# One plain pair fewer in front of the seven-product feed-forward, a new opening order, and an embedding unit moved behind it

## The chip, the cores and the metric

The kernel runs on one core of a Trainium2 chip. The metric is device time in microseconds (us): 2044.14 us, the median of 3 runs (2043.42 to 2046.07). TensorE multiplies (PE in the profile; its weight loads are PEld), VectorE (DVE), ScalarE (ACT) and GpSimd (POOL) do the element-wise work, SyncE (SP) issues most transfers.

## The reference, cut to what matters

One layer of a decoder trunk on 1024 prompt tokens and 64 sample tokens, model width 1024. After two mixing branches and an output projection come the feed-forward and an embedding term:

```
x = x + merged @ w_o
up = rmsnorm(x, g_ffn) @ w_up              # 1024 -> 2*3072
gate, val = split(causal_dwconv3(up))
x = x + (gelu(gate) * val) @ w_down        # 3072 -> 1024
e = rmsnorm(p @ w_ple, g_ple)              # p: 256 wide, known from the start
x = x + sigmoid(x @ w_ple_gate) * e
```

## The kernel before, in words

Channels lie on the partitions, tokens along the rows. The tokens are done in two halves, one whole layer after the other: the first has 512 prompt tokens, the second 512 prompt and 64 sample tokens (576, in two groups of 288). Each fp32 product is made of three fp32r products, high by high, high by low and low by high; so every weight block (128x128) gives three matmuls per group of tokens.

Weights come in units of 1024 columns (eight blocks), in an order fixed in the list `ORDER`. Each unit is loaded five units ahead by SP (`load`), and two units ahead ACT makes its high part (`split_hi`, tile whi, L324) and DVE its low part (`split_lo`, tile wlo, L329); `hook` issues these three from inside the unit that is being multiplied.

The feed-forward has 24 pairs f of a gate block and a value block. `PLAN` gives the order of its work, as a list that `ffn_plan` writes out:

- ("ple", j): half of the embedding product p @ w_ple, one unit. Each of its four results is copied out by ACT, stored to DRAM by a DMA that ACT issues, squared by ACT, and the square is added to a running sum by POOL (`j_ple`, `square`, L442). After unit 1 a job starts (`stat_later`) that turns the sum into a row of reciprocal roots with two small groups of matmuls (L453, L487) and DVE work between them (L468, L478).
- ("up", u): one up-projection block done plainly, one unit of 8 x 3 matmuls per group. A plain pair is two such units.
- ("step", f, p): product p of 7 of pair f. The pairs after the first PLAIN are done by a scheme for 2x2 block matrices with seven products instead of eight: the two blocks of weights (gate, value) by two halves of the input channels on one side, two halves of the channels by two halves of the tokens on the other. A step is half a unit (4 blocks, 12 matmuls over half of the tokens); two steps share a unit. Products 1 and 2 take the weights as they are, and rows of the normalised input as they are (b11, b21). The products 3, 5, 6 and 7 need sums of weights (made early in DRAM by `make_sums`), and 4 to 7 need sums of the input (t1 to t4, made by the job `operands`).
- ("down", d): one unit of the down-projection, 19 of them among the steps, the last five behind them.

Jobs (`Job`) are Python generators that are advanced by one `tick` after each block of a whole unit and after each second block of a step; what a job issues is put into the queues of the engines in this order, and each engine works its queue in order. At the start of the feed-forward three of them run beside the matmuls: `stat2` (waits 8 ticks, then L453, 6 ticks, L468 and L478, 7 ticks, L487), `operands` (starts at tick 10, four rounds of 11 ticks, DVE L1121 to L1125 and L1107, ACT L1115, L1119 and L1105), and for each finished up-block `j_up`: the evacuation on DVE (L503, or L505 to L507 in the second half), one tick later a first tap of the convolution on ACT (L529), two ticks later two more on DVE (L533).

In `step`, product 1 starts a PSUM bank, and when its four blocks are issued ACT copies the bank to a row (L1181); product 2 is then added into the same bank by the matmuls, so it has to follow that copy. In the order before, product 2 is the last of its pair.

Of the kernel before, what the change touches and what calls it, by code (L numbers as in the profile page):

```python
# [48 lines left out]
def paired(a, b, lead):  # L49
    o = [(a, m) for m in range(lead)]  # L50
    for m in range(8):
        o.append((b, m))
        if m + lead < 8:
            o.append((a, m + lead))
    return o
# [9 lines left out]
SUMS = ("s1", "s2", "s3", "s4")  # L65
CHUNK = 4

PLAIN = 4


def ffn_plan():

    plan, steps, down = [("ple", 0), ("ple", 1)], 0, 0
    plan += [("up", s * FF + f) for f in range(PLAIN) for s in range(2)]
    for f in range(PLAIN, FF):
        todo = [(f, 1), (f, 6)] + [(f - 1, 3)] * (f > PLAIN) + [(f, p) for p in (7, 5, 4, 2)]
        ready = min(f - 4, down + 2)
        for i, x in enumerate(todo):
            plan.append(("step", *x))
            steps += 1  # L80
            while i >= len(todo) - 2 and steps % 2 == 0 and down < ready:
                plan.append(("down", down))
                down += 1
    plan.append(("step", FF - 1, 3))
    assert steps % 2
    return plan, down


PLAN, DOWNS = ffn_plan()


def slot_order(hf):

    o = [("lx", m) for m in range(8)]
    o += [("q", i) for i in range(4)] + [("k", i) for i in range(4)]
    o += [("v", i) for i in range(8)]
    o += [("lg", m) for m in range(8)]
    o += paired("ga", "ya", LEAD_A)
    o += [("rg", m) for m in range(8)]
    o += paired("gb", "yb", LEAD_B)  # L100
    o += [("wo", m) for m in range(8)]
    first = None
    for what, *x in PLAN:
        if what != "step":
            o.append((what, *x))
        elif first is None:
            first = tuple(x)
        else:
            o.append(("halves", first, tuple(x)))
            first = None  # L110
    assert first is None
    o += [("down", f) for f in range(DOWNS, FF)]
    o += [("gate", m) for m in range(8)] * (1 + hf)
    return o


ORDER = slot_order(0) + slot_order(1)
NU = len(ORDER)
PACKED = [(n, i) for n, c in (("lx", 8), ("q", 4), ("k", 4), ("v", 8), ("lg", 8), ("ga", 8), ("ya", 8), ("rg", 8), ("gb", 8), ("yb", 8), ("wo", 8)) for i in range(c)]
# [19 lines left out]
class Job:  # L139
# [7 lines left out]
    def step(self):  # L147
        try:
            self.wait += next(self.gen) or 1
        except StopIteration as e:  # L150
            self.done, self.val = True, e.value
# [16 lines left out]
class Trunk:  # L168
# [974 lines left out]
    def step(self, H, X, prep, rb, P, f, p):  # L1143

        nc = self.nc
        n = H.T // 2
        if self.half is None:
            i, h = self.cur, 0
            self.cur += 1
            self.half = i  # L1150
        else:
            i, h = self.half, 1
            self.half = None
        assert ORDER[i][0] == "halves" and ORDER[i][1 + h] == (f, p)
        s = P.setdefault(f, {})
        chain = {1: "a", 2: "a", 3: "c", 5: "c"}.get(p, p)
        if chain not in s:
            s[chain] = self.ps_new(1)[0]
            first = True
        else:  # L1160
            first = False
        bank = s[chain]
        out = bank[:, 0:n]
        xs = X[PRODUCTS[p][1]]
        for kk in range(4):
            b = 4 * h + kk
            while len(xs) <= kk:
                prep.step()
            xh, xl = xs[kk]
            wh, wl = self.whi[i % RING][:, b], self.wlo[i % RING][:, b]  # L1170
            mm = nc.tensor.matmul
            mm(out, lhsT=wh, rhs=xh, start=first and kk == 0, stop=False, skip_group_check=True)  # L1172
            mm(out, lhsT=wh, rhs=xl, start=False, stop=False, skip_group_check=True)  # L1173
            mm(out, lhsT=wl, rhs=xh, start=False, stop=kk == 3, skip_group_check=True)  # L1174
            if kk % 2:
                self.tick()
            self.hook(i, b)
        V = nc.vector
        if p == 1:
            s["row"] = self.new()  # L1180
            nc.scalar.copy(s["row"][:, 0:n], out)  # L1181
            return
        row = s["row"]
        r1, r2 = row[:, 0:n], row[:, n:2 * n]
        if p == 2:
            s["xg"] = self.new(wide=True)
            self.prefix(H, s["xg"], self.stf[:, f], 2)
            s["c11"] = self.start(self.j_first(H, rb, s["xg"], s.pop("a")))
        elif p == 6:
            V.tensor_add(r2, out, r1)  # L1190
            self.ps_rel([s.pop(6)])
        elif p == 7:
            V.tensor_add(r1, out, r2)
            self.ps_rel([s.pop(7)])
        elif p == 5:
            s["v"] = self.new()
            V.scalar_tensor_tensor(s["v"][:, n:2 * n], out, -1.0, r1, op0=ALU.mult, op1=ALU.subtract)
        elif p == 4:
            V.tensor_sub(s["v"][:, 0:n], out, r1)  # L1199
            self.ps_rel([s.pop(4)])  # L1200
            xv = self.new(wide=True)
            self.prefix(H, xv, self.stf[:, FF + f], 2)
            s["val"] = self.start(self.j_value(H, rb, s["v"], xv, FF + f))
        else:
            V.tensor_add(r2, out, r2)  # L1205
            self.ps_rel([s.pop("c")])
            gate = self.start(self.j_gelu(H, rb, row, s["c11"], s["xg"], f))
            s["hp"] = self.start(self.j_val(H, s["val"], gate), delay=6 if f == FF - 1 else 9)
# [181 lines left out]
    def run(self, H, res, nxt):  # L1390
# [10 lines left out]
        first = None if H.hf else self.first_units(H, xn, res["w"])  # L1401
# [27 lines left out]
        for g in range(4):  # L1429
            banks = self.ps_new(len(H.chunks))  # L1430
            for j in range(2):
                i = self.begin(("v", 2 * g + j))
# [97 lines left out]
        emb = None  # L1530
        for what, *x in PLAN:
            if what == "step":
                if x == [PLAIN, 1]:
                    prep.get()
                    self.rel(x1p[:4])
                    for r in x1p[4:]:
                        for name, h in (("b21", slice(0, n)), ("b22", slice(n, T))):
                            X[name].append(tuple(y[:, h] for y in r.get()))
                self.step(H, X, prep, rb, P, *x)
            elif what == "up":  # L1540
                self.up(H, *x, x1p, rb, P)
            elif what == "ple":
                self.ple(H, *x, pp, esum)
                if x == [1]:
                    emb = self.start(self.stat_later(H, esum), delay=10)
            else:
                self.down(H, *x, P, x1)
# [23 lines left out]
        for i, g in enumerate(parts):  # L1571
# [4 lines left out]
            first = self.gates_abreast(x2p, groups) if i == 0 else []  # L1576
# [307 lines left out]
```

## Time and profile before

| what | value |
|---|---|
| median of 3 runs | 2044.14 us |
| the profiled execution's own time | 2044.08 us |
| its span, first to last instruction | 2042.3 us |
| PE busy | 2022.4 us, 99% |
| DVE, ACT, POOL busy | 1444.7, 908.7, 580.8 us |
| chain that ended last: PE, DVE, ACT, POOL | 88%, 6%, 2%, 0% |
| TensorE clock granted, mean | 0.996 of full |

The profile is one execution. Busy matmuls overlap, so the time that a matmul takes from PE is read from the distance between starts. The first half's feed-forward begins about 498 us into the span, the second's about 1530 us. Times in rows are from the start of the span.

### The profile page before, as it was taken

The numbers are of one execution on the slowest core, as the hardware profiler recorded it, in microseconds if no ns is written. First come the engines' busy times: TensorE is split into PE (matmuls) and PEld (weight loads), VectorE is DVE, ScalarE is ACT, GpSimd is POOL, SyncE is SP. The second block draws the span as 40 slices with busy tenths as digits, with TensorE's granted clock in tenths as the row PEclk, the third lists the DMA queues.
The fourth block names the chain that finished last, engine by engine and source line by source line (L and its number), as shares of the span: only waits on it lengthen the run. The fifth ranks groups of instructions, "written<-read, shape, count | busy, mean of one in ns | idle before, by whom it ended". The sixth has DMA issues, their size and how long they took to land.

```text
span 2042.3 us, 33650 instructions
## 1 busy us (share of the span) xinstructions
PE 2022.4 (99%) x13360; PEld 1892.5 (93%) x13360; DVE 1444.7 (71%) x2132; ACT 908.7 (44%) x1298; POOL 580.8 (28%) x750
## 2 busy tenths in 40 slices
PE   9999999999999999999999999999999999999997
PEld 7798888888799999989999999989999999999997
DVE  7986445655898888888884533545447888888887
ACT  5554324425654444444463321423237444444444
POOL 4751223303232222203541001441024233333302
PEclk9999999999999999999999999999999999999998
DMA  8699975794355444453322222222333444444443
GB/s 282 152 249 288 229 189 165 185 237 144 104 166 155 154 156 148 151 197 110 117 95 78 91 83 73 71 96 83 106 119 109 123 138 134 143 135 135 134 157 131
DMA packets 123998, 296.87 MB, mean 145 GB/s; under 512 B 12096, under 2 KB 14528, under 8 KB 123840
## 3 DMA queue, kind: packets, MB, share of 16 engines
q1 hardware_dynamic: 108000, 264.42, 39.6%
q0 software_dynamic: 12672, 25.17, 7.6%
q10 hardware_dynamic: 3168, 5.14, 0.7%
q8 instruction: 104, 1.70, 0.3%
q14 instruction: 54, 0.44, 0.1%
HBM read 282.56 MB, written 62.46 MB: 169 GB/s over the span
## 4 chain that ended last, share of the span: by engine, by line
PE 88%; DVE 6%; issue 2%; ACT 2%; DMA 1%; POOL 0%; ACTq 0%; SPq 0%; DVEq 0%; POOLq 0%
PE bank L335 58%; PE bank L1174 7%; PE bank L1173 7%; PE bank L1172 7%; DVE wlo L329 2%; PE bank L1441 2%; PE bank L1439 2%; PE bank L1440 2%; DVE row L533 1%; PE bank L874 1%; PE bank L886 1%; PE bank L852 1%; PE bank L876 1%; ACT row L529 1%; PE bank L990 0%
## 5 line engine op out<-in xcount | busy, mean ns | idle before, releaser
L335 PE MATMUL bank<-row,whi 128*128 128x288 f32 (+3 forms) x5440 | 1206.1, 329 | 0.0
L335 PEld LDWEIGHTS bank<-row,whi 128*128 128x128 f32 x5440 | 874.3, 189 | 70.2 <-issue 0.9
L335 PE MATMUL bank<-row,wlo 128*128 128x288 f32 (+3 forms) x2720 | 750.4, 327 | 0.0
L329 DVE TENSOR_TENSOR wlo<-raw,whi 128x1024 fp32r<-128x1024 f32 x390 | 507.6, 1302 | 151.1 <-ACT whi L324 149.5
L324 ACT CAST whi<-raw 128x1024 fp32r<-128x1024 f32 x390 | 407.4, 1045 | 321.5 <-issue 109.6
L335 PEld LDWEIGHTS bank<-row,wlo 128*128 128x128 f32 x2720 | 465.6, 188 | 36.2 <-DVE wlo L329 0.5
L1174 PE MATMUL bank<-row,wlo 128*128 128x256 f32 (+1 forms) x1120 | 323.7, 289 | 0.0
L1173 PE MATMUL bank<-row,whi 128*128 128x256 f32 (+1 forms) x1120 | 323.6, 289 | 0.0
L1172 PE MATMUL bank<-row,whi 128*128 128x256 f32 (+1 forms) x1120 | 323.3, 289 | 0.0
L1172 PEld LDWEIGHTS bank<-row,whi 128*128 128x128 f32 x1120 | 212.6, 190 | 0.8
L1173 PEld LDWEIGHTS bank<-row,whi 128*128 128x128 f32 x1120 | 212.5, 190 | 0.8
L1174 PEld LDWEIGHTS bank<-row,wlo 128*128 128x128 f32 x1120 | 212.5, 190 | 0.2 <-DVE wlo L329 0.2
L533 DVE SCALAR_TENSOR_TENSOR row<-row,vec,row 128x512 f32<-128x512 f32 (+2 forms) x224 | 184.4, 823 | 20.0 <-ACT row L529 16.0
L417 DVE TENSOR_TENSOR row<-bank,row 128x288 f32<-128x288 f32 (+1 forms) x144 | 72.5, 531 | 153.8 <-PE bank L335 151.5
L442 POOL TENSOR_TENSOR row<-row,row 128x576 f32<-128x576 f32 (+2 forms) x47 | 78.1, 1661 | 345.9 <-ACT row L438 345.5
L529 ACT ACTIVATE row<-row,vec 128x512 f32<-128x512 f32 (+2 forms) x112 | 95.1, 850 | 111.2 <-DVE row L507 36.1
L398 ACT CAST row<-row 128x512 fp32r<-128x512 f32 (+1 forms) x132 | 84.2, 642 | 101.9 <-DVE row L422 31.7
L1261 POOL TENSOR_TENSOR row<-row,row 128x256 f32<-128x256 f32 (+2 forms) x60 | 44.4, 754 | 296.9 <-DVE row L1205 296.9
L400 DVE TENSOR_TENSOR row<-row,row 128x512 fp32r<-128x512 f32 (+1 forms) x132 | 106.0, 804 | 30.1 <-ACT row L398 28.8
L1248 POOL TENSOR_TENSOR row<-row,row 128x512 f32<-128x512 f32 (+1 forms) x60 | 66.0, 1114 | 150.7 <-DVE row L1199 150.7
L422 DVE TENSOR_TENSOR row<-bank,row 128x288 f32<-128x288 f32 (+1 forms) x168 | 82.4, 527 | 29.0 <-PE bank L335 29.0
L1441 PE MATMUL bank<-whi,row 128*128 128x256 f32 (+1 forms) x288 | 81.2, 282 | 0.0
(182 smaller groups left out, 1999.2 us busy)
## 6 DMA issues: line engine op xcount, KB each, us to landing
raw<-wpk SPq DMA_DIRECT2D x250, 512.0 KB, 3.6
raw<-sums SPq DMA_DIRECT2D x160, 256.0 KB, 3.1
raw<-wpk SPq DMA_DIRECT2D x120, 256.0 KB, 3.1
sums<-wpk SPq DMA_DIRECT2D x24, 1024.0 KB, 10.4
sums<-wpk POOLq DMA_DIRECT2D x12, 1024.0 KB, 13.1
sums<-sums POOLq DMA_DIRECT2D x12, 1024.0 KB, 12.8
row<-xB SPq DMA_DIRECT2D x24, 288.0 KB, 4.6
row<-xA SPq DMA_DIRECT2D x16, 256.0 KB, 5.2
```

What stands on the lines that cost most here:

```text
L324: self.nc.scalar.copy(self.whi[i % RING], self.raw[i % RAW])
L329: self.nc.vector.tensor_sub(self.wlo[j], self.raw[i % RAW], self.whi[j].bitcast(F32))
L335: self.nc.tensor.matmul(b[:, 0:g.stop - g.start], lhsT=w, rhs=x[:, g], start=s, stop=e)
L398: nc.scalar.copy(hi[:, 0:H.T], row[:, 0:H.T])
L400: nc.vector.tensor_sub(lo[:, 0:H.T], row[:, 0:H.T], hi[:, 0:H.T].bitcast(F32))
L422: self.nc.vector.tensor_add(row[:, g], b[:, 0:H.n], row[:, g])
L529: nc.scalar.activation(t[:, 0:n], xf[:, 0:n], AF.Identity, bias=bcol, scale=wcol(0))
L533: nc.vector.scalar_tensor_tensor(t[:, 0:n], xf[:, j:j + n], wcol(j), t[:, 0:n], op0=ALU.mult, op1=ALU.add)
L1172: mm(out, lhsT=wh, rhs=xh, start=first and kk == 0, stop=False, skip_group_check=True)
L1173: mm(out, lhsT=wh, rhs=xl, start=False, stop=False, skip_group_check=True)
L1174: mm(out, lhsT=wl, rhs=xh, start=False, stop=kk == 3, skip_group_check=True)
L1441: nc.tensor.matmul(b, lhsT=xl, rhs=wh[:, ws], start=False, stop=j == 1 and kk == 3)
```

## The change: three plain pairs instead of four, a new order for the first two pairs of the scheme, one embedding unit later

The constant `PLAIN` goes from 4 to 3, so pair 3 is done by the scheme. Only ("ple", 0) stands ahead of the up-blocks; ("ple", 1) follows the eight steps with which the scheme opens. The opening mixes pairs 3 and 4: products 1 of both, 2 of both, then 6, 7, 5, 4 of pair 3; behind the embedding unit come 6 of pair 4, 3 of pair 3, and 7, 5, 4 of pair 4. From pair 5 on the order within a pair is as before. There are 147 steps instead of 140 in each half; the last of them has a unit of its own. The weights' list grows from 78 to 80 units for ups and steps in each half.

```diff
-PLAIN = 4
+PLAIN = 3
...
-    plan, steps, down = [("ple", 0), ("ple", 1)], 0, 0
+    plan, steps, down = [("ple", 0)], 0, 0
     plan += [("up", s * FF + f) for f in range(PLAIN) for s in range(2)]
+    f = PLAIN
+
+    opening = [(f, 1), (f + 1, 1), (f, 2), (f + 1, 2), (f, 6), (f, 7), (f, 5), (f, 4)]
+    second = [(f + 1, 6), (f, 3), (f + 1, 7), (f + 1, 5), (f + 1, 4)]
     for f in range(PLAIN, FF):
-        todo = [(f, 1), (f, 6)] + [(f - 1, 3)] * (f > PLAIN) + [(f, p) for p in (7, 5, 4, 2)]
+        todo = {PLAIN: opening, PLAIN + 1: second}.get(f) or [(f, 1), (f, 6), (f - 1, 3)] + [(f, p) for p in (7, 5, 4, 2)]
...
+        if f == PLAIN:
+            plan.append(("ple", 1))
     plan.append(("step", FF - 1, 3))
-    assert steps % 2
...
-    assert first is None
+    if first is not None:
+        o.append(("halves", first))
...
-            self.half = i
+            self.half = i if len(ORDER[i]) == 3 else None
...
-                if x == [PLAIN, 1]:
+                if x == [PLAIN, 6]:
                     prep.get()
                     self.rel(x1p[:4])
+                if x == [PLAIN, 1]:
                     for r in x1p[4:]:
```

## Rows read from the trace of the kernel before

**Rows 1.** The profile's page, engines and costliest groups: busy us, mean ns of one.

```profile
PE 2022.4 (99%) x13360; PEld 1892.5 (93%) x13360; DVE 1444.7 (71%) x2132; ACT 908.7 (44%) x1298; POOL 580.8 (28%) x750
...
L329 DVE TENSOR_TENSOR wlo<-raw,whi 128x1024 fp32r<-128x1024 f32 x390 | 507.6, 1302 | 151.1 <-ACT whi L324 149.5
...
L533 DVE SCALAR_TENSOR_TENSOR row<-row,vec,row 128x512 f32<-128x512 f32 (+2 forms) x224 | 184.4, 823 | 20.0 <-ACT row L529 16.0
```

**Rows 2.** Timeline of PE, first half: start us, duration us, count, idle before and releaser.

```profile
504.85 0.72 PE L335 MATMUL bank<-row,whi 128*128 128x512 f32 x2
...
516.54 0.50 PE L487 MATMUL bank<-row,ones 128*128 128x512 f32 x1 [2.31 <-DVE row L478]
...
558.58 0.28 PE L1172 MATMUL bank<-row,whi 128*128 128x256 f32 x1
...
576.15 0.63 PE L335 MATMUL bank<-row,whi 128*128 128x512 f32 x2
...
581.62 0.28 PE L1172 MATMUL bank<-row,whi 128*128 128x256 f32 x1
...
593.13 0.63 PE L335 MATMUL bank<-row,whi 128*128 128x512 f32 x2
```

**Rows 3.** Timeline of PE, second half.

```profile
1536.44 0.80 PE L335 MATMUL bank<-row,whi 128*128 128x288 f32 x4
...
1549.03 0.98 PE L487 MATMUL bank<-row,ones 128*128 128x512 f32 x3 [1.69 <-DVE row L478]
...
1619.86 0.70 PE L335 MATMUL bank<-row,whi 128*128 128x288 f32 x4
...
1626.26 0.29 PE L1172 MATMUL bank<-row,whi 128*128 128x288 f32 x1
...
1638.97 0.69 PE L335 MATMUL bank<-row,whi 128*128 128x288 f32 x4
```

**Rows 4.** Windows: us, busy PE, PEld, DVE, ACT, POOL, granted clock, DMA share, GB/s.

```profile
1549.00:1553.00 4.00, 3.98 (x16) 3.66 (x17) 3.94 (x5) 3.32 (x7) 4.00 (x2) 0.57 0.10 17
```

**Rows 5.** Timeline of DVE, first half.

```profile
511.61 1.78 DVE L468 TENSOR_TENSOR row<-cst,rstd 128x512 fp32r<-128x512 f32 x1
513.42 3.06 DVE L478 SCALAR_TENSOR_TENSOR row<-cst,rstd,row 128x128 fp32r<-128x128 f32 x4
...
517.84 2.08 DVE L329 TENSOR_TENSOR wlo<-raw,whi 128x1024 fp32r<-128x1024 f32 x1 [0.15 <-ACT whi L324]
...
526.93 0.68 DVE L468 TENSOR_TENSOR row<-cst,rstd 128x512 fp32r<-128x512 f32 x1
527.65 1.14 DVE L478 SCALAR_TENSOR_TENSOR row<-cst,rstd,row 128x128 fp32r<-128x128 f32 x4
...
548.49 0.68 DVE L503 TENSOR_TENSOR row<-bank,row 128x512 f32<-128x512 f32 x1
```

**Rows 6.** Timeline of POOL, first half.

```profile
511.36 3.18 POOL L442 TENSOR_TENSOR row<-row,row 128x512 f32<-128x512 f32 x2 [2.42 <-ACT row L438]
```

**Rows 7.** Timeline of ACT, first half, at the scheme's first product.

```profile
562.54 0.82 ACT L529 ACTIVATE row<-row,vec 128x512 f32<-128x512 f32 x1 [0.23 <-DVE row L503]
563.26 0.36 ACT L1181 COPY row<-bank 128x256 f32<-128x256 f32 x1
```

**Rows 8.** Timeline of DVE, second half.

```profile
1540.51 1.69 DVE L1121 TENSOR_TENSOR row<-row 128x288 f32<-128x288 f32 x1
...
1544.67 1.92 DVE L468 TENSOR_TENSOR row<-cst,rstd 128x512 fp32r<-128x512 f32 x1
...
1546.65 2.51 DVE L478 SCALAR_TENSOR_TENSOR row<-cst,rstd,row 128x128 fp32r<-128x128 f32 x5
...
1562.98 1.32 DVE L478 SCALAR_TENSOR_TENSOR row<-cst,rstd,row 128x128 fp32r<-128x128 f32 x5
1564.23 0.44 DVE L1121 TENSOR_TENSOR row<-row 128x288 f32<-128x288 f32 x1
...
1585.53 0.45 DVE L505 TENSOR_TENSOR row<-bank,row 128x288 f32<-128x288 f32 x1
```

## The prediction, made before the changed kernel ran

> **What bounds the kernel now.** Read the page's engine line first: PE is busy for 99% of the span [rows 1]. So what counts is how many matmul slots there are, and where PE stands still. The timeline of PE gives the slots by the distance of starts, and names each stop and its releaser. In the feed-forward's beginning there are two stops: 2.31 us in the first half and 1.69 us in the second, both at the matmuls that spread the reciprocal roots (L487), both for DVE's L478 [rows 2, 3]. The timeline of DVE says why it was late: four L478 take 3.06 us and one L468 takes 1.78 us there, and 1.14 and 0.68 us for the same work 14 us later [rows 5]. At the slow place POOL was adding squares of the embedding (two adds in 3.18 us, from 511.36) [rows 6]. Last come the windows: right behind the stop of the second half PE had a granted clock of 0.57 over 4 us, so most of it at the lower level, 1.2 GHz [rows 4].
>
> The second thing to see is lag. The fifth up-block of the first half is evacuated at 548.49 [rows 5]. PE had finished it three units before the steps began at 558.58 [rows 2], and a unit is 5.47 us, so at 542.2: DVE is 6.3 us behind. It costs nothing, for PSUM has free banks and the low parts of weights are made two units ahead. When the steps begin, the copy of the first product still runs at 563.26, behind L529, which had waited for a DVE evacuation [rows 7]. That product ended at 560.0 (558.58 plus 1.44), so ACT is 3.2 us late there, and nobody waits: in the old order product 2 comes four steps later.
>
> **The change, part by part.**
>
> *The pair that changes its form.* First half: a unit of 24 matmuls takes 581.62 - 576.15 = 5.47 us, eight steps take 593.13 - 581.62 = 11.51 us, so 1.439 us each [rows 2]. A plain pair is 2 x 5.47 = 10.94 us, seven steps are 10.07 us: 0.87 us saved. Second half: a unit 1626.26 - 1619.86 = 6.40 us, a step (1638.97 - 1626.26) / 8 = 1.589 us [rows 3]: 12.80 - 11.12 = 1.68 us. Sum: -2.55 us. The list has two more units in each half, so two more low parts on DVE (1.30 us each [rows 1]) and as many high parts on ACT; they lie beside matmuls. The odd last step has a unit of 1.44 us for itself, with 5.47 us of a down unit behind it: nothing. If that cover were gone it would be at most those two splits, 2.6 us per half; I take 0.
>
> *The embedding unit that is moved.* Its matmuls are the same wherever they stand. With it go four copies, four stores issued from ACT's queue, four squares on ACT, four adds on POOL, and the job of the embedding's roots. In their old place they leave L468 and L478 undisturbed: these should take 0.68 and 1.14 us, end near 513.7, and L487 finds them done, for PE comes there at 504.85 plus 13 blocks of 0.684 us, 513.7. So 2.31 and 1.69 us go, 4.0 us, and with the second stop the stretch of low clock: 4.00 x (1 - 0.57) = 1.7 us [rows 2 to 4]. Nothing else is late in their place: the first up-block follows, and its eighth block, the only one that needs the last row of the output projection, comes seven blocks after the start. Bounds: none of it goes (0), or all of it (-5.7); the value I take is all, since the rows 14 us apart differ only by what POOL does. In the new place the four adds slow DVE, and four copies and squares hold ACT, in a stretch with steps around; there DVE has just had a stop of PE to catch up (below), and the unit itself needs one split in 5.47 us. L487 of the embedding comes 13 ticks after its L453 as before. I take 0; its ends are nothing and the 4.0 us of the two stops that the same adds caused before.
>
> *The wait that is added.* In the opening, product 2 of pair 3 follows two steps after product 1 began, and adds into the bank that ACT must first copy. Copy and product are queued so: the copy is issued on ACT after L529 of the sixth (now last) up-block, and that L529 waits on DVE for the evacuation. Behind the copy on ACT stand the next split and the copy for pair 4; behind product 2 on PE stands everything. So the question is when DVE reaches that sixth evacuation.
>
> First half. PE reaches the steps at 504.85 + 48 blocks x 0.684 + 0.46 (two L487) = 538.1. DVE: in the old trace the fifth evacuation ends at 549.17, with all four rounds of `operands` before it, and the ticks of these rounds do not move. I take from it what is no longer in that queue: the slowing of L468, L478 and one L329 (1.10 + 1.92 + 0.78 against the mean of 1.30) = 3.8 us, and the embedding's L468 and L478, 1.8 us. I add one evacuation (0.68), one pair of taps (2 x 0.82) and one low part of a product (about an evacuation, 0.68), which now fall before the same tick, 3.0 us [rows 1, 5]. The sixth evacuation ends at 546.6. L529 and the copy need 0.82 + 0.36 [rows 7]: 547.7. Product 2 could start at 538.1 + 2 x 1.44 = 541.0. Stop: 6.7 us.
>
> Second half, the same way. The steps are reached at 1536.44 + 48 x 0.80 + 0.98 = 1575.8 [rows 3]. The fifth evacuation starts at 1585.53 and ends, in three pieces of about twice the first's 0.45, at 1586.4. Off: the slowing of three subtractions of 1.55 to 1.69 us against 0.44 (one stands), 3.5 us, of L468 1.24 and of L478 1.19; the embedding's own 2.0 [rows 5, 8]. On: 0.9 + 1.65 + 0.7. It ends at 1581.8, the copy at 1582.9; product 2 could start at 1575.8 + 3.18 = 1579.0. Stop: 3.9 us.
>
> Bounds of these two: below, DVE stands where it stands when the steps begin in the old trace. There the copy ends at 563.62, 5.04 us behind 558.58, against the 2.88 us that the two steps give: 2.2 us in the first half, and nothing in the second, where two steps give 3.18 us. Above, none of the slowing goes away: 10.5 and 9.8 us. I take 6.7 and 3.9, nearest to the rows of DVE at the same tick.
>
> **Sum.** -2.55 - 4.0 - 1.7 + 6.7 + 3.9 = +2.35 us. The profiled execution took 2044.08 us (a span of 2042.3 and 1.8 around it), 0.06 below the median of the runs, so forecast and comparison can go by either: 2044.08 + 2.35 = 2046.4 us. What a measurement of this kernel can tell from no change is about 0.2%, 4.1 us; the forecast lies inside it.
>
> **Rivals.**
>
> *The new stops take the clock with them: slower.* The mechanism: PE stands still before product 2 in both halves, and the matmuls behind it run at 1.2 GHz for a while. The price is that of the one stretch in the trace, 1.7 us for each stop [rows 4], so +3.4: 2049.8 us. It decides from one such fall on: 2.35 + 1.7 = 4.05 is the edge of what can be told. For it: the old stop of 1.69 us has the low clock right behind it [rows 3, 4], and both new ones are longer. Against it: the stop of 2.31 us had none, and the second new one might be short. The Trainium skill ("TensorE: Matmul & The Clock Gate", section "HAM oscillation — how this bites in real kernels") says that waits of PE between groups of matmuls throttle it again, so that the next group starts cold; by that rule both stops would be followed by a fall, while the rows show one fall for two stops. By the rule the sum is +5.75, by the rows' better half +2.35.
>
> *DVE is through in time: faster.* With POOL quiet, the rounds of `operands` run without holes, and the copy is as late as at the old beginning of the steps: stops of 2.2 and 0 us. Sum: -2.55 - 5.7 + 2.2 = -6.05, 2038.0 us. For it: most of the lag of 6.3 us was built where DVE was slowed. Against it: in the old kernel DVE had three more up-units, 16 us, to catch up after the last round, and now the last round ends two ticks before the steps.
>
> *Only the arithmetic shows.* The roots' stops stay or come back at the moved embedding unit, and no new stop appears: -2.55, 2041.5 us. Against it: it needs DVE fast in the one place and slow in the other.
>
> **How the numbers follow.** Forecast 0.42, clock 0.33, DVE in time 0.18, arithmetic alone 0.07. The forecast and the last lie within 0.2%: same 0.49; slower 0.33; faster 0.18. The range must reach toward both sides: down to 2038.8, which leaves out half of the fast case, and up to 2052.0, 2.2 us above the clock rival, for stops longer than worked out (with the upper bounds it would be 2056). The likeliest case's own range is 2043 to 2049.
>
> **What would show it.** In the profile after: PE stops in L1172 of product 2 of pair 3, released by ACT's L1181, one in each half, near 541 and 1570 to 1580 us; no stop at L487 in the first 15 us of either feed-forward, with L468 near 0.68 us; steps at 1.44 and 1.59 us as before; 2.55 us fewer matmul slots. If product 2 starts without a wait, the lag is read wrongly and the fast rival holds. If the granted clock is below 1.00 behind the stops, it is the slow one. If L487 still waits for L478, the moved unit was not the cause.

## The result and the profile after

The changed kernel takes 2057.45 us (median of 4 runs, 2056.96 to 2057.85), the kernel before 2044.11 beside it: a ratio of 1.0065 [1.0052, 1.0077], 13.3 us slower. The forecast was +2.35 with a range up to 2052.0. The profiled execution took 2057.14 us, 13.06 above the one before; its span is 2055.4 us, and the first feed-forward starts 0.5 us later in it.

The page's engine line, to be held against [rows 1]:

```profile
PE 2022.3 (98%) x13384; PEld 1894.0 (92%) x13384; DVE 1448.3 (70%) x2140; ACT 912.0 (44%) x1304; POOL 588.9 (29%) x756
```

PE is busy for the same time in a span 13.1 us longer, and this busy time hides slow matmuls. Of its 24 more matmuls, 36 are added in the first half (two units of 24 become seven steps of 12) and 12 go in the second (two units of 48, the same steps): the slots are those of the forecast. So the rest is stops and clock. The largest of PE's waits in the two feed-forwards' beginnings (engine, line, releaser: us in total, times, longest), first 500 to 700 us, then 1530 to 1700 us:

```profile
PE bank L1178 <- ACT row L1187: 7.2, 1, 7.2
...
PE bank L1178 <- ACT row L1187: 5.4, 1, 5.4
```

L1178 and L1187 are the lines L1172 and L1181 of before, L493 is L487, L341 is L335. It is product 2 of pair 3 behind ACT's copy, once in each half, as the prediction placed it. Its surroundings in the timeline of PE:

```profile
514.35 0.63 PE L493 MATMUL bank<-row,ones 128*128 128x512 f32 x2
...
541.27 0.28 PE L1179 MATMUL bank<-row,whi 128*128 128x256 f32 x1
541.39 0.28 PE L1180 MATMUL bank<-row,wlo 128*128 128x256 f32 x1
548.84 0.58 PE L1178 MATMUL bank<-row,whi 128*128 128x256 f32 x1 [7.17 <-ACT row L1187]
...
554.08 0.28 PE L1178 MATMUL bank<-row,whi 128*128 128x256 f32 x1
...
584.57 0.50 PE L493 MATMUL bank<-row,ones 128*128 128x512 f32 x1 [0.76 <-DVE row L484]
...
1554.77 0.96 PE L493 MATMUL bank<-row,ones 128*128 128x512 f32 x4
...
1592.54 0.61 PE L1178 MATMUL bank<-row,whi 128*128 128x288 f32 x1 [5.42 <-ACT row L1187]
...
1598.47 0.32 PE L1178 MATMUL bank<-row,whi 128*128 128x288 f32 x1
...
1633.16 0.83 PE L493 MATMUL bank<-row,ones 128*128 128x512 f32 x3 [1.27 <-DVE row L484]
...
1638.55 0.66 PE L341 MATMUL bank<-row,whi 128*128 128x288 f32 x3 [1.01 <-DVE row L1205]
```

Read the distance of starts. Ahead of the stop matmuls of 256 columns follow each other by 0.120 us; behind it 24 of them take 554.08 - 548.84 = 5.24 us, 0.218 each. At 0.120 they would take 2.88: 2.36 us lost. In the second half 24 of 288 columns take 5.93 us where 24 x 0.133 = 3.20 would do: 2.73 lost. At 514.35 and 1554.77 the roots' L493 no longer waits ([rows 2, 3] had 2.31 and 1.69 us there). The rows at 584.57 and 1633.16 are the roots of the moved embedding unit; the last is the down-projection unit behind them, which waits for a bank that DVE empties late. The windows give the clock (busy PE, PEld, DVE, ACT, POOL, granted clock, DMA share, GB/s):

```profile
503.66:548.84 45.18, 38.01 (x188) 32.04 (x186) 35.59 (x58) 31.18 (x51) 9.49 (x17) 0.94 0.27 92
541.50:548.80 7.30, 0.17 (x2) 0.00 (x0) 5.65 (x8) 4.86 (x8) 1.72 (x3) 0.66 0.10 27
548.84:554.08 5.24, 5.24 (x24) 5.24 (x25) 3.40 (x5) 1.78 (x3) 1.41 (x3) 0.51 0.75 244
1542.17:1586.96 44.79, 44.79 (x338) 44.28 (x336) 34.76 (x67) 30.23 (x49) 11.91 (x26) 1.00 0.25 87
1592.54:1598.47 5.93, 5.93 (x25) 5.93 (x25) 3.71 (x6) 1.87 (x4) 3.49 (x7) 0.50 0.65 217
```

Behind the two stops the clock is 0.51 and 0.50, the lower level, 1.2 GHz. From the second feed-forward's first small matmuls (L459, 1542.17) to its stop the clock is 1.00, so the fall of [rows 4] is gone. The first row goes from the same matmuls of the first half (503.66) to product 2: 45.18 us pass where PE has 38.01 us of work, and DVE is busy for 35.59 and ACT for 31.18 of them, so the busy time of neither would have filled PE's time. The second row is the stop itself: DVE is busy for 5.65 and ACT for 4.86 of 7.30 us, so neither is full; they wait for each other. That is to be seen in their timelines, DVE first:

```profile
512.15 0.69 DVE L474 TENSOR_TENSOR row<-cst,rstd 128x512 fp32r<-128x512 f32 x1
512.87 1.14 DVE L484 SCALAR_TENSOR_TENSOR row<-cst,rstd,row 128x128 fp32r<-128x128 f32 x4
...
543.74 0.69 DVE L1113 TENSOR_TENSOR row<-row,row 128x512 fp32r<-128x512 f32 x1 [1.62 <-ACT row L1111]
544.35 1.53 DVE L539 SCALAR_TENSOR_TENSOR row<-row,vec,row 128x512 f32<-128x512 f32 x2
...
546.93 0.68 DVE L509 TENSOR_TENSOR row<-bank,row 128x512 f32<-128x512 f32 x1
```

```profile
545.92 0.63 ACT L1236 ACTIVATE row<-row 128x512 f32<-128x512 f32 x1 [2.21 <-DVE row L539]
...
547.72 0.81 ACT L535 ACTIVATE row<-row,vec 128x512 f32<-128x512 f32 x1 [0.23 <-DVE row L509]
548.44 0.62 ACT L1187 COPY row<-bank 128x256 f32<-128x256 f32 x2
```

The roots' work runs at 0.69 and 1.14 us, the quick values of [rows 5]. The last round of sums (L1113) waits for ACT's cast, the taps (L539) come behind it, ACT's L1236 waits 2.21 us for the taps, then a low part, then the sixth evacuation, done at 547.61; L535 (L529 of before) and the copy follow. It is the chain of the forecast, 1.0 us later.

The account, after less before: slots -2.55; roots' stops -4.0; the low clock behind the second -1.65; new stops 7.17 + 5.42 = +12.6; low clock behind them +5.1; waits behind the moved unit 0.76 + 1.27 + 1.01 = +3.0; the later start +0.5. Sum +13.0, of 13.06 measured.

### The profile page after: what moved, and what is told of

Its sections match the earlier page's. It is cut to its first block, busy times and chain, and to the rows that moved or that the text cites. A ratio compares the mean times of both kernels' runs of the same rounds, so it can differ in the third digit from the quotient of the medians.

```text
span 2055.4 us, 33750 instructions
## 1 busy us (share of the span) xinstructions
PE 2022.3 (98%) x13384; PEld 1894.0 (92%) x13384; DVE 1448.3 (70%) x2140; ACT 912.0 (44%) x1304; POOL 588.9 (29%) x756
## 3 DMA queue, kind: packets, MB, share of 16 engines
q8 instruction: 105, 1.72, 0.3%
## 4 chain that ended last, share of the span: by engine, by line
PE 84%; DVE 9%; issue 3%; ACT 2%; POOL 1%; DMA 1%; ACTq 0%; SPq 0%; DVEq 0%; POOLq 0%
PE bank L341 54%; PE bank L1178 7%; PE bank L1180 7%; PE bank L1179 7%; DVE wlo L335 3%; DVE row L539 2%; PE bank L1446 2%; PE bank L1447 2%; PE bank L1445 2%; PE bank L880 1%; PE bank L892 1%; ACT row L535 1%; PE bank L858 1%; DVE row L406 1%; PE bank L882 1%
## 5 line engine op out<-in xcount | busy, mean ns | idle before, releaser
L341 PE MATMUL bank<-row,whi 128*128 128x288 f32 (+3 forms) x5344 | 1184.6, 329 | 1.2 <-DVE row L1205 1.0
L341 PEld LDWEIGHTS bank<-row,whi 128*128 128x128 f32 x5344 | 858.1, 189 | 70.4 <-DVE row L1205 1.2
L341 PE MATMUL bank<-row,wlo 128*128 128x288 f32 (+3 forms) x2672 | 737.5, 327 | 0.2 <-DVE wlo L335 0.2
L335 DVE TENSOR_TENSOR wlo<-raw,whi 128x1024 fp32r<-128x1024 f32 x394 | 512.1, 1300 | 155.4 <-ACT whi L330 154.1
L341 PEld LDWEIGHTS bank<-row,wlo 128*128 128x128 f32 x2672 | 457.1, 188 | 35.8 <-DVE wlo L335 0.9
L1178 PE MATMUL bank<-row,whi 128*128 128x256 f32 (+1 forms) x1176 | 342.6, 291 | 12.6 <-ACT row L1187 12.6
L1180 PE MATMUL bank<-row,wlo 128*128 128x256 f32 (+1 forms) x1176 | 342.5, 291 | 0.0
L1179 PE MATMUL bank<-row,whi 128*128 128x256 f32 (+1 forms) x1176 | 342.3, 291 | 0.0
L1178 PEld LDWEIGHTS bank<-row,whi 128*128 128x128 f32 x1176 | 225.6, 192 | 13.9 <-ACT row L1187 13.0
L539 DVE SCALAR_TENSOR_TENSOR row<-row,vec,row 128x512 f32<-128x512 f32 (+2 forms) x224 | 185.4, 828 | 22.7 <-ACT row L535 18.7
L535 ACT ACTIVATE row<-row,vec 128x512 f32<-128x512 f32 (+2 forms) x112 | 95.1, 850 | 125.0 <-POOL row L1267 41.4
L1267 POOL TENSOR_TENSOR row<-row,row 128x256 f32<-128x256 f32 (+2 forms) x63 | 48.9, 789 | 291.7 <-DVE row L1211 291.7
L1254 POOL TENSOR_TENSOR row<-row,row 128x512 f32<-128x512 f32 (+1 forms) x63 | 71.1, 1143 | 167.7 <-DVE row L1205 164.1
L1446 PE MATMUL bank<-wlo,row 128*128 128x256 f32 (+1 forms) x288 | 81.4, 283 | 0.5 <-DVE wlo L335 0.5
```

The lines of the kernel that those rows point to most:

```text
L335: self.nc.vector.tensor_sub(self.wlo[j], self.raw[i % RAW], self.whi[j].bitcast(F32))
L341: self.nc.tensor.matmul(b[:, 0:g.stop - g.start], lhsT=w, rhs=x[:, g], start=s, stop=e)
L535: nc.scalar.activation(t[:, 0:n], xf[:, 0:n], AF.Identity, bias=bcol, scale=wcol(0))
L539: nc.vector.scalar_tensor_tensor(t[:, 0:n], xf[:, j:j + n], wcol(j), t[:, 0:n], op0=ALU.mult, op1=ALU.add)
L1446: nc.tensor.matmul(b, lhsT=xh, rhs=wl[:, ws], start=False, stop=False)
```

## Experiments

Before stands in brackets; ratios carry their interval. The question is why DVE and ACT are late at product 2: because the opening asks for the copy too early, because the unit was moved, because of when the last round of sums is issued, or because the two engines, with their waits for each other, need more time in this stretch than PE's work covers.

**The unit back in front.**

```diff
-    plan = [("ple", 0)]
+    plan = [("ple", 0), ("ple", 1)]
...
-        if f == PLAIN:
-            plan.append(("ple", 1))
```

> The changed kernel with the second embedding unit back in front of the up-blocks (three plain pairs and the new opening stay). Theory LAG (VectorE is about 8 us behind when the steps begin, because the last round of the input sums ends two ticks before them): VectorE gets one unit more to catch up; by the old trace its sixth evacuation is then about 5 us behind in the first half and 3 us in the second, so product 2 of pair 3 stops TensorE for about 4.0 and 1.3 us instead of 7.2 and 5.4; the old stops at the spreading of the reciprocal roots (2.3 and 1.7 us) and their low clock come back; about 2049.5 us. Rival UNIT (the moved embedding unit is what costs): no stop at product 2 longer than 2.2 us, about 2041.5 to 2043.7 us.

2051.20 us [2045.24], 1.0029 [1.0019, 1.0039]. Timeline of PE:

```profile
517.87 0.50 PE L491 MATMUL bank<-row,ones 128*128 128x512 f32 x1 [2.31 <-DVE row L482]
...
556.76 0.58 PE L1176 MATMUL bank<-row,whi 128*128 128x256 f32 x1 [3.21 <-ACT row L1185]
...
1557.09 0.84 PE L491 MATMUL bank<-row,ones 128*128 128x512 f32 x3 [1.72 <-DVE row L482]
...
1598.91 0.40 PE L1176 MATMUL bank<-row,whi 128*128 128x288 f32 x1 [1.07 <-ACT row L1185]
```

The roots' stops are back (2.31 and 1.72 us, where [rows 2, 3] have 2.31 and 1.69), so the unit made them. The stops at product 2 shrink to 3.21 and 1.07 us but stay. PE is now at product 2 by 556.76 - 3.21 = 553.55, 11.9 us later than in the changed kernel (548.84 - 7.17 = 541.67), and the copy only 7.9 us later (556.76 against 548.84): the unit in front was cover for DVE and ACT as well as work for them. Each beside its own runs of the kernel before, the changed kernel is 13.3 us slower and this one 6.0: moving the unit accounts for about 7 of the 13 us, not for the rest.

**Product 2 put last in the opening.**

```diff
-    opening = [(f, 1), (f + 1, 1), (f, 2), (f + 1, 2), (f, 6), (f, 7), (f, 5), (f, 4)]
+    opening = [(f, 1), (f + 1, 1), (f, 6), (f, 7), (f, 5), (f, 4), (f, 2), (f + 1, 2)]
```

> The changed kernel with products 2 of pairs 3 and 4 at the end of the opening, so nothing waits for the copy of product 1 early. Theory LAG: VectorE is late for everything, so TensorE stops at the second step unit for the low part of its weights, which in the changed kernel's trace is ready at 547.0 and 1590.4 us: stops of about 5.3 and 3.3 us, released by the split on VectorE, low clock behind them; about 2053 us. Rival COPY (only the new dependency on ScalarE's copy costs, the lag is harmless as in the old kernel): no stop over 1 us, no low clock, 2057.4 - 12.6 - 5.3 = 2039.5 us.

2052.12 [2045.24], 1.0031 [1.0019, 1.0043]. Timeline of PE:

```profile
543.23 0.39 PE L1178 MATMUL bank<-row,whi 128*128 128x256 f32 x1 [1.56 <-ACT whi L330]
...
547.06 0.58 PE L1180 MATMUL bank<-row,wlo 128*128 128x256 f32 x1 [3.32 <-DVE wlo L335]
```

No wait for the copy is left, and PE stands still all the same (3.09 us in the second half), now for the split weights that stand in the same two queues. The copy is only the first thing asked of late engines; that the order alone is the cause is refuted. It changes how much is lost: 6.9 us over the kernel before here, 13.3 in the changed kernel.

**The sums issued earlier.**

```diff
-        prep = self.start(self.operands(H, x1, x1p, X, held), delay=10)
+        prep = self.start(self.operands(H, x1, x1p, X, held), delay=2)
```

> The changed kernel with the input sums (operands) started at tick 2 of the feed-forward instead of tick 10. Theory LAG: VectorE stood idle for 5.6 us at 503 to 510 us; the rounds end 8 ticks (5.4 and 6.4 us) earlier, so the stops at product 2 shrink to about 2 and 0 us and the clock falls at most once: 2041 to 2043 us. Rival COPY (the place of the copy in ScalarE's queue behind the last up-block decides, wherever the sums stand): stops stay within 1 us of 7.2 and 5.4, 2056 to 2058 us. A third way: the sums' work on ScalarE delays the copies of the output projection and TensorE stops earlier instead.

2054.99 [2045.24], 1.0044 [1.0029, 1.0059]: a miss. Timeline of PE, then of DVE:

```profile
543.00 0.58 PE L1180 MATMUL bank<-row,wlo 128*128 128x256 f32 x1 [3.30 <-DVE wlo L335]
...
549.58 0.38 PE L1178 MATMUL bank<-row,whi 128*128 128x256 f32 x1 [1.52 <-ACT row L1187]
...
1589.99 0.61 PE L1178 MATMUL bank<-row,whi 128*128 128x288 f32 x1 [4.24 <-ACT row L1187]
```

```profile
539.66 0.69 DVE L1113 TENSOR_TENSOR row<-row,row 128x512 fp32r<-128x512 f32 x1 [2.40 <-ACT row L1111]
...
547.68 0.68 DVE L509 TENSOR_TENSOR row<-bank,row 128x512 f32<-128x512 f32 x1
```

The last round is done 4 us sooner (539.66 against 543.74), and the sixth evacuation is not sooner at all (547.68 against 546.93). So the tick of the last round does not decide.

**The unit moved in the kernel before, and nothing else.**

```diff
-    plan = [("ple", 0), ("ple", 1)]
+    plan = [("ple", 0)]
...
+        if f == PLAIN:
+            plan.append(("ple", 1))
```

> The kernel before (four plain pairs, old order of products) with only the second embedding unit moved behind the six steps of pair 4. Theory LAG: the two stops at the roots and the low clock go (-5.7), the embedding's later roots and banks cost up to 3.1 as in the changed kernel, the steps begin 8 ticks sooner after the last round, which may cost 0 to 3 us at low parts of weights: 2041 to 2045 us. Rival UNIT (the moved unit is what costs): 2050 us or more.

2047.12 [2045.24], 1.0009 [1.0000, 1.0019]: no gain, a miss. Timeline of PE:

```profile
547.44 0.50 PE L337 MATMUL bank<-row,wlo 128*128 128x512 f32 x1 [2.37 <-DVE wlo L331]
...
1609.61 0.67 PE L337 MATMUL bank<-row,whi 128*128 128x288 f32 x3 [1.63 <-ACT row L429]
```

The roots' stops are gone as forecast, and the gain is handed back 30 us and more later: in low parts that DVE makes late (2.37 us, and three short waits of 1.6 us together), and at the unit's own copies (L429). Part of the second half's loss is a low clock that has another origin (last section).

**The changed kernel again, and with its stop filled.** The second kernel puts matmuls of ones into a bank that nobody reads ahead of product 2:

```diff
+        if (f, p) == (PLAIN, 2):
+            fill = self.ps_new(1)
+            for _ in range(32 if H.hf else 48):
+                nc.tensor.matmul(fill[0][:, 0:n], lhsT=self.ones, rhs=X["b11"][0][0], start=True, stop=True)
+            self.ps_rel(fill)
```

> The changed kernel itself, on the chip that also runs the next three, as their base: about 13 us over the kernel before, stops at product 2 of pair 3 of 7.2 and 5.4 us, low clock behind both.

> The changed kernel with 48 (second half 32) matmuls of ones into a free bank put between product 1 of pair 4 and product 2 of pair 3: work that nothing reads and that fills most of the stop (about 5.8 and 4.3 us). Theory CLOCK (the low clock behind the stops costs 2.6 + 2.9 us, and comes because TensorE stands still): the granted clock stays at full speed through both places and the time falls by about 5.5 us against the changed kernel. Rival: the fall of the clock costs little or has another cause; the time stays within 1 us, and the filling may even delay product 2.

Again: 2057.68 [2044.56], 1.0063 [1.0045, 1.0081], stops of 7.15 and 5.41 us. Filled: 2054.58 (2052.53 to 2059.27), 1.0052 [1.0035, 1.0069]. Timeline of PE, then windows of the filled kernel:

```profile
553.74 0.39 PE L1183 MATMUL bank<-row,whi 128*128 128x256 f32 x1 [1.51 <-ACT row L1192]
...
1596.68 0.40 PE L1183 MATMUL bank<-row,whi 128*128 128x288 f32 x1 [1.16 <-ACT row L1192]
```

```profile
553.80:559.00 5.20, 5.20 (x44) 5.20 (x45) 4.88 (x8) 2.69 (x4) 1.35 (x3) 1.00 0.77 249
1547.00:1551.00 4.00, 4.00 (x21) 4.00 (x22) 1.87 (x4) 3.60 (x7) 3.62 (x3) 0.64 0.30 118
1596.70:1601.00 4.30, 4.30 (x32) 4.30 (x33) 4.26 (x8) 2.16 (x4) 3.47 (x7) 1.00 0.68 212
```

PE is as late for the copy as before (553.74 - 508.56 = 45.18 us behind the feed-forward's first small matmuls, as 548.84 - 503.66), but the clock behind is 1.00. In the profile the stretch from these matmuls in the first half to those in the second is 1544.81 - 508.56 = 1036.25 us, against 1542.17 - 503.66 = 1038.51 in the changed kernel: 2.26 less, where 2.36 had been lost at the low clock. In the second half this profile has a fall of another origin (the row from 1547; last section), which the repeated changed kernel has too. Against that one the stretch from the small matmuls (1544.81 and 1542.29) to the end of the span (2057.5 and 2057.1) is 2.1 us shorter, where 2.73 had been lost. So the fall is the stop's, and its price is real time.

The whole times say less. The median gained 3.1 of the 5.1 us, but single times overlap (2052.53 to 2059.27 against 2057.10 to 2058.86), and the profiled execution is the slowest of its four: it came to the first feed-forward 4.9 us late (508.56 against 503.66). So the place and the size are read from the traces; by the medians alone the gain is not clear of noise.

**Taps and halves of the last four up-blocks later.**

```diff
+DEFER = {1: 30, FF + 1: 23, 2: 17, FF + 2: 10}
...
-        yield 1
+        yield DEFER.get(u, 1)
```

The same delay is given to the job that joins the halves.

> The changed kernel with the convolution of the last four up-blocks (and what follows it) issued 10 to 30 ticks later, behind the copies of product 1; their evacuations stay where they are. Theory WORK (what has to go through VectorE and ScalarE ahead of the copy and of the second step unit's low part is too much for the time): about four pairs of taps, two multiplications and their waits leave the queue, 6 to 8 us; stops fall to 0 to 2 us, no low clock, and the time to 2041 to 2045 us on a chip where the changed kernel takes 2057. Rival (only the one first tap directly ahead of the copy matters): stops fall by about 1 us each, 2054 us. A cost that may come: the convolutions now meet the moved embedding unit's copies on ScalarE, 0 to 3 us.

2052.13 [2044.56], 1.0040 [1.0026, 1.0053]: a miss. Timeline of PE:

```profile
565.61 0.39 PE L1179 MATMUL bank<-row,whi 128*128 128x256 f32 x1 [2.81 <-ACT whi L331]
...
1625.83 0.50 PE L494 MATMUL bank<-row,ones 128*128 128x512 f32 x1 [1.53 <-DVE row L475]
```

Both stops at product 2 are gone, and PE stands still later instead: for a high part that ACT makes behind the moved unit's copies and a tap that was put off, and at the moved unit's roots. That the work put off makes these waits is likely and not shown by itself.

**Three of the four rounds of sums left out.** The first round's operands stand in for the other three, so the products of those rows are not the reference's; matmuls and their order stay.

```diff
         for k in range(4):
+            if k:
+                for name in ("b11", "t1", "t2", "t3", "t4"):
+                    X[name].append(X[name][0])
+                yield 11
+                continue
```

> The changed kernel with three of the four rounds of input sums left out (the first round's rows stand in for the others, so the scheme's products 4 to 7 and product 1 are not the reference's). Theory WORK: about 8.6 us of VectorE and as much of ScalarE leave the stretch ahead of the steps, both stops go and with them the low clock: 12.6 + 5.5 us less than the changed kernel, about 2039 us. Rival (the up-blocks' own work makes VectorE late, the sums only use gaps): stops of over 3 us remain.

2041.31 [2044.56], 0.9982 [0.9972, 0.9992], 3.25 us faster. Windows around the places of the two stops, and between them one of a fall of the clock elsewhere:

```profile
540.00:556.00 16.00, 16.00 (x118) 15.20 (x117) 12.93 (x17) 9.39 (x13) 5.75 (x7) 1.00 0.58 184
1536.97:1540.38 3.41, 3.41 (x16) 3.41 (x15) 1.55 (x1) 3.20 (x6) 3.41 (x3) 0.50 0.26 101
1580.00:1600.00 20.00, 20.00 (x153) 20.00 (x152) 13.11 (x18) 11.71 (x20) 9.06 (x13) 1.00 0.56 191
```

At both places PE is busy throughout and the clock is 1.00. With less work for DVE and ACT the same order of matmuls runs through. The gain is less than the slots and the roots' stops together (2.55 + 5.65 = 8.2 us): the three waits behind the moved unit stay, 3.0 us in this profile, and the clock falls once with no stop ahead of it (the middle row, 1.7 us; last section). That leaves 3.5.

**The parts by themselves.** Three plain pairs in the old order (the first); the embedding's adds on POOL thirteen ticks later and its roots six ticks later, in the kernel before (the second); both (the third); four plain pairs in the new order (the fourth, the changed kernel with `PLAIN = 4`). The diffs are those of the first two:

```diff
-PLAIN = 4
+PLAIN = 3
```

```diff
-        yield from self.square(e[:, 0:H.T], esum[:, 0:H.T], m)
-        self.rel(e)
+        g = self.square(e[:, 0:H.T], esum[:, 0:H.T], m)
+        for _ in g:
+            self.rel(e)
+            yield 13
+        if m == 0:
+            self.rel(e)
...
-                    emb = self.start(self.stat_later(H, esum), delay=10)
+                    emb = self.start(self.stat_later(H, esum), delay=16)
```

> The kernel before with three plain pairs instead of four and nothing else: both embedding units in front, the old order of products (product 2 last). Theory WORK: the roots' stops and their low clock stay (6.0 us with it), 2.55 us of slots go, and the steps begin 5 us nearer to the sums than in the kernel before, so the second step unit waits 0.5 to 2 us for its low part in the first half: -2.5 to +0.5 us against the kernel before. Rival (taking the fourth plain pair away is what breaks the cover): +3 us or more.

> The kernel before with the embedding's adds on GpSimd issued 13 ticks later (and its roots 6 ticks later): same units, same order. Theory WORK, part on the roots: L468 and L478 run undisturbed, the stops of 2.3 and 1.7 us and the low clock behind the second go, -6.0 us; the adds now slow VectorE a little later, which gives back 0 to 3 us: 2038 to 2042 us where the kernel before takes 2044.5. Rival: what is taken from the roots comes back in full as waits for low parts, as when the unit was moved alone (x4): 0 to +2 us.

> z1 and z2 together: three plain pairs, old order, both units in front, the adds later. If the two are independent, the sum of their two effects (about -4 to -8 us). If the lag of VectorE is the common limit, less than the better of the two.

> The changed kernel with four plain pairs again: the new opening (of pairs 4 and 5) and the moved unit stay. Theory WORK: VectorE has two up-units (11 and 13 us) more than in the changed kernel to work off the sums, so product 2 stops TensorE for about 2.5 to 4 us in the first half and 0 to 1 in the second, low clock at most once: +2 to +6 us against the kernel before. Rival (the new order costs by itself, whatever stands ahead): stops of 7 and 5 us as in the changed kernel, +13 + 2.5 us.

All beside 2044.56. Three plain pairs, old order: 2048.12, 1.0018 [1.0009, 1.0028], a miss. Adds later: 2050.35, 1.0030 [1.0020, 1.0040], a miss. Both: 2053.85, 1.0047 [1.0032, 1.0061], the sum of the two, where a gain was expected. Four plain pairs, new order: 2048.35, 1.0018 [1.0009, 1.0027], 3.8 us slower, inside the expected 2 to 6. Timelines of PE, one fence for each of first, second and fourth:

```profile
516.98 0.50 PE L487 MATMUL bank<-row,ones 128*128 128x512 f32 x1 [2.33 <-DVE row L478]
...
554.09 0.39 PE L1174 MATMUL bank<-row,wlo 128*128 128x256 f32 x1 [1.20 <-DVE wlo L329]
```

```profile
528.95 1.23 PE L453 MATMUL bank<-cst,row 128*128 128x1 f32 x5 [3.36 <-POOL row L442]
```

```profile
547.23 0.50 PE L341 MATMUL bank<-row,wlo 128*128 128x512 f32 x1 [2.38 <-DVE wlo L335]
...
558.04 0.39 PE L1178 MATMUL bank<-row,whi 128*128 128x256 f32 x1 [2.62 <-ACT row L1187]
...
1599.04 0.40 PE L1178 MATMUL bank<-row,whi 128*128 128x288 f32 x1 [2.65 <-ACT row L1187]
```

Without the new order, a plain pair less is 3.6 us slower, not 2.55 faster: low parts are late at once, and the roots' stop of the first half stays. With four plain pairs the new order still stops at product 2, for 2.62 and 2.65 us (0 to 1 us was expected in the second half), where three give 7.17 and 5.42. With the adds later the roots' stop of the first half shrinks from 2.31 us to two waits of 0.6, but the embedding's own sum (L453) then waits for the adds, 3.36 us there and 2.23 in the second half, and the clock is low behind both (0.50 over 529 to 533, 0.74 over 1567 to 1571). None of these is faster than the kernel before; the only one that is leaves work out.

## Why the prediction was wrong

Place, mechanism and releaser were right, and so was the sign of the likeliest case; the size was not: +2.35 against +13.1.

- *Slots, -2.55*: right (0.120 and 0.133 us a matmul, and the counts above).
- *Roots' stops and the low clock behind the second, -5.7*: right where it was looked for; putting the unit back in front brings the stops back. "Nothing else is late in their place" held for the first blocks only: moving the unit alone gained nothing in all.
- *Stops at product 2, 6.7 and 3.9*: 7.17 and 5.42, 2.0 us short in sum, 0.5 in the first half and 1.5 in the second. The sixth evacuation of the first half was forecast for 546.6 and ended at 547.6, half of that by the later start. The forecast took "what is no longer in that queue" off DVE's total, as if DVE had no holes; the rows show 1.62 us of waiting for ACT in that stretch, and ACT 2.21 us for DVE. That these holes are what was missed is likely; piece by piece it is not shown.
- *The step that failed: that no clock falls behind the new stops.* It stood as a rival at 0.33, with 1.7 us a stop, the price of the one stretch in [rows 4]. Both stops had the fall, and it cost 2.36 and 2.73 us, as the low stretch was 5.24 and 5.93 us long, not 4 us at 0.57. The argument against it, that the stop of 2.31 us had none, spoke of a stop less than half as long. The Trainium skill ("TensorE: Matmul & The Clock Gate", section "HAM oscillation — how this bites in real kernels") says that waits between groups of matmuls start the next group cold; both stops agree (0.51 and 0.50 behind them). Of the two stops in its rows, one with a fall and one without, the forecast took the one without for both new stops; the rule was the better guide for stops of this length.
- *The embedding unit in its new place: "I take 0"*: 3.0 us in three waits, within the bound of 4.0; with the unit back in front none of the three is there. It was not the adds that the forecast feared: in the first half they end at 571.1, and L474, which takes the part of L468, runs at 582.3 in its quick 0.68 us. The roots come late because DVE has no slack there: it is busy for 15.78 of the 16.00 us from 576.

These three and the later start are the difference: 2.0 + 5.1 + 3.0 + 0.5 = 10.6 of 10.7 us.

Behind the mis-sized stops is one cause that the experiments settle: in the stretch between the feed-forward's start and the steps, DVE and ACT need, with their waits for each other, more time than PE gives them (45.18 us for 38.01, though DVE is busy for 35.59 of them). Moving the waiting product, the sums, the taps, or the unit moves the stop; only less work takes it away. Leaving the sums out takes away busy time and waits together, so how much of the lag is either stays open.

## What to carry to other kernels

Work that a busy engine is spared is worth nothing if it was the cover of another's backlog: before cutting matmuls, ask how far the evacuating engines lag there and what they must deliver next. A lag shared by two engines that wait for each other isn't the sum of one engine's durations; add the holes. Price a new stop of a saturated TensorE with the stretch at 1.2 GHz behind it, and take that stretch from stops of a like length.

## What was not expected of the hardware

The clock also falls with no stop at all. In the changed kernel run again, the twenty small matmuls of L459 ran as in the first (2.16 us, at 1542.29 and 1542.17), with PE busy throughout; in the first run the clock behind them was 1.00 (1542 to 1547), in the second:

```profile
1544.00:1548.00 4.00, 4.00 (x21) 3.97 (x21) 1.39 (x3) 3.60 (x8) 3.14 (x3) 0.57 0.43 168
```

The same fall is in the profile of the unit moved alone:

```profile
1539.00:1543.00 4.00, 4.00 (x21) 3.98 (x20) 1.66 (x3) 3.60 (x8) 3.39 (x3) 0.57 0.45 170
```

It costs about 4.00 x (1 - 0.57) = 1.7 us. A fall at this place, with PE busy, is in seven of the fourteen profiles, of kernels with three and with four plain pairs: so two profiles can differ by 1.7 us whatever the edit did. Nor does a stop's length alone decide: behind the roots' stop of 2.31 us the kernel before had 1.00 (516.5 to 520), and with the unit back in front, behind a stop of the same 2.31 us:

```profile
517.90:521.50 3.60, 3.60 (x11) 2.83 (x12) 3.44 (x4) 3.57 (x7) 2.95 (x2) 0.66 0.09 31
```

And with four plain pairs, behind the longer stop of 2.62 us:

```profile
558.00:561.50 3.50, 3.46 (x28) 3.46 (x29) 3.46 (x6) 1.54 (x3) 1.45 (x4) 1.00 0.78 255
```

Likewise the stop of 1.69 us in the kernel before has a fall behind it [rows 3, 4], and the stop of 1.72 us with the unit back in front has none (1.00 over 1557 to 1560.5). What decides between these cases stays open.
